# A hybrid attention layer on one core: the first half of the output projection is evicted by ScalarE, and x joins in an accumulating DMA

## The chip, the cores and the metric

The kernel runs on one core of a Trainium2 chip. A core has five engines with their own instruction queues: TensorE (PE) for matrix products, VectorE (DVE) and ScalarE (ACT) for elementwise work, GpSimd (POOL) for small elementwise work, and SyncE (SP), which here issues nearly all DMAs. Each queue runs in order; an instruction that waits holds all that stand behind it. The metric is the device time of one execution in microseconds (us); the profile comes from one execution that the hardware profiler recorded.

## What is computed

One layer of a decoder on 2048 rows of 1024 channels: an RMS norm, one input projection, three attention branches whose outputs stand side by side (512 + 256 + 256 channels), a gate, and an output projection that is added to x:

```python
def reference(x, mem, positions, ...):
    h = rms_norm(x, norm_g[l])
    proj = h @ w_in[l]
    cq, ckv, kr, dq, dk, dv, mq, z = jnp.split(proj, IN_OFFSETS, axis=-1)
    y_mla = mla_branch(...)      # 8 heads, channels 0 to 511 of y
    y_diff = diff_branch(...)    # 4 heads, 2 softmax maps each, channels 512 to 767
    y_mem = mem_branch(...)      # 4 heads against 256 memory tokens, channels 768 to 1023
    y = jnp.concatenate([y_mla, y_diff, y_mem], axis=-1) * jax.nn.silu(z)
    return x + y @ w_out[l]
```

## The kernel before

The rows are cut into 4 blocks of 512, each of 4 tiles of 128 rows. The branches run one after the other as steps: memory (m), differential (d, two groups), latent (a, four groups), each over the 4 blocks. A step is prepared (projections, norms, rotation, transposes by DMA, row maxima) and then runs its maps: scores `st` on PE (L890 to L894), the exponential on ACT (L492), its low part `plo` on DVE (L493), and the products with the values (L502 to L505). A product in full precision is three products of fp16 parts, so one [128, 512] tile of the output projection over four channel tiles of 128 is 12 matmuls (L930 to L932).

The output projection is split in two halves by channels. `out_dm` takes the four channel tiles of the differential and memory branches. For each of the 16 row tiles it loads the rows of x into a buffer `xr` (L945), adds the product to each half of it (`out_tile`, with the addition on DVE at L933), and stores it to the DRAM scratch `part` (L950). `out_a` takes the latent branch's four channel tiles for blocks 0 to 2: it loads the rows of `part` into `xa` (L960), adds the product (L933), and stores the result to `out` (L965). `xr`, `xa` and the staged rows of w_out share two buffers (tag `f4`). The last block is held on chip: `out_last` loads four tiles `acc` of `part` (L981), adds three of the four channel tiles to half of them, and `out_tail` does the rest after the last map and stores it (L1002). The products go to two PSUM tiles `pp`.

The order of the work is a list of tasks. The maps have positions in time worked out from their costs; each preparation and each filling task (`out_dm`, `out_a`, `out_last`) has a span of such positions over which it is spread by the costs that it yields. `out_dm` is spread from shortly before the first latent step to 20 positions before the fourth group, `out_a(b)` and `out_last` lie beside the last steps. Each task's instructions get a priority, and the framework puts them into the queues in an order that it takes from these priorities and a simulated timeline, so each engine's order is fixed when the kernel is built, and is made anew when an instruction changes.

Other places that the prediction speaks of: `prep_a` makes keys and queries of a latent step: POOL's memsets (L853, L859), addition (L835), rotation (L340 to L344) and power (L101), DVE's scalings (L845, L846), and SP's transposes of keys (`kT_a`, L856) and queries (`qB_a`, L864 and L873).

Of the kernel before, what the change touches and what calls it, by code (L numbers as in the profile page):

```python
# [16 lines left out]
ALU = mybir.AluOpType  # L17
# [23 lines left out]
def hybrid_block(ctx: ExitStack, tc: tile.TileContext, x, mem, positions, norm_g, w_in, mla_q_norm_g,  # L41
# [21 lines left out]

# [1 line left out]
    ident = cst.tile([P, P], BF16, name="ident")  # L65
# [37 lines left out]

# [1 line left out]
    def stage(name, pool=None):  # L105
# [10 lines left out]
    def load(dst, src, pace=PACE):  # L116
        """At the start, loads take turns with the transposes on the DMA queues."""
        if 0 < len(turned) < 2 * NPACE:
            with tc.issue_after(turned[max(0, len(turned) - pace)].ins):
                SP.dma_start(dst, src)  # L120
        else:
            SP.dma_start(dst, src)
# [18 lines left out]

# [1 line left out]
    def load_w(w, cols, gains, name, out, pool=None, ahead=2, pace=PACE):  # L143
        """Column ranges of w as fp16 pairs: NK views [P, 2, n] appended to out."""
        n = sum(c for _, c in cols)
        kpu = 2 if n > 256 else 4

        def fetch(i):
            st = stage(f"wst_{name}{i}", pool).rearrange("p (k c) -> p k c", k=2)
            at = 0  # L150
            for c0, c in cols:
                load(st[:, :, at:at + c], w[0, 2 * i * P:(2 * i + 2) * P, c0:c0 + c].rearrange("(k p) c -> p k c", p=P), pace)
                at += c
            return st

        sts = [fetch(i) for i in range(ahead - 1)]
        yield 1.0
        for i in range(NK // 2):
            if i + ahead - 1 < NK // 2:
                sts.append(fetch(i + ahead - 1))  # L160
                yield 1.0
            st = sts[i]
            if 2 * i % kpu == 0:
                wt = bigt([P, kpu, 2, 1024 // kpu], f"w_{name}{i}")
            for k in range(2):
                g = gains[:, 2 * i + k:2 * i + k + 1]
                dst = wt[:, (2 * i + k) % kpu]
                A.activation(dst[:, 0, :n], st[:, k, :n], AF.Copy, scale=g)
                V.scalar_tensor_tensor(dst[:, 1, :n], st[:, k, :n], g, dst[:, 0, :n], ALU.mult, ALU.subtract)
                out.append(dst)  # L170
            yield 1.0
# [8 lines left out]
    def project_block(hts, units, n, dst):  # L180
        """dst: [P, 4, >= n]"""
        for t in range(4):
            ps = ps_p.tile([P, 512], F32, tag="pp", name="pp")
            project(ps, hts[t], units, n)
            A.activation(dst[:, t, 0:n], ps[:, :n], AF.Copy, scale=1.0 / WS)
            yield 0.01 * n
# [6 lines left out]

# [1 line left out]
    top = tc.cur_priority  # L195
# [50 lines left out]

# [1 line left out]
    cos_t = cst.tile([P, NT, 16], F32, name="cos_t")  # L248
# [63 lines left out]
    def rope_tabs(b, g, name):  # L312
        """cos and sin of block b's tokens with the halves of the gain folded in."""
        tb = wk.tile([P, 2, 4, 32], F32, tag="rtab", name=f"rt_{name}", bufs=1)
        c = cos_t[:, 4 * b:4 * b + 4, :]
        s = sin_t[:, 4 * b:4 * b + 4, :]
        g1, g2 = _bc(g[:, 0:16], 1, 4), _bc(g[:, 16:32], 1, 4)
        G.tensor_tensor(tb[:, 0, :, 0:16], c, g1, ALU.mult)
        G.tensor_tensor(tb[:, 0, :, 16:32], c, g2, ALU.mult)
        G.tensor_tensor(tb[:, 1, :, 0:16], s, g2, ALU.mult)  # L320
        G.tensor_tensor(tb[:, 1, :, 16:32], s, g1, ALU.mult)
        return tb

    def rope(dst, src, tb, nh, eng, name):
        """dst, src: [P, 4, nh, 32]"""
        tmp = tmp4(f"rtmp_{name}")[:, 0:128 * nh].rearrange("p (t h d) -> p t h d", t=4, d=32)
        C = _bc(tb[:, 0], 2, nh)
        Sn = _bc(tb[:, 1], 2, nh)
        eng.tensor_tensor(dst, src, C, ALU.mult)
        eng.tensor_tensor(tmp[..., 0:16], src[..., 16:32], Sn[..., 0:16], ALU.mult)  # L330
        eng.tensor_tensor(tmp[..., 16:32], src[..., 0:16], Sn[..., 16:32], ALU.mult)
        eng.tensor_tensor(dst[..., 0:16], dst[..., 0:16], tmp[..., 0:16], ALU.subtract)
        eng.tensor_tensor(dst[..., 16:32], dst[..., 16:32], tmp[..., 16:32], ALU.add)

    def rope_in_place(q, tb, nh, eng, tmp):
        """q: [P, 4, nh, 32]"""
        tmp = tmp.rearrange("p (t h d) -> p t h d", t=4, d=32)
        C = _bc(tb[:, 0], 2, nh)
        Sn = _bc(tb[:, 1], 2, nh)
        eng.tensor_tensor(tmp[..., 0:16], q[..., 16:32], Sn[..., 0:16], ALU.mult)  # L340
        eng.tensor_tensor(tmp[..., 16:32], q[..., 0:16], Sn[..., 16:32], ALU.mult)
        eng.tensor_tensor(q, q, C, ALU.mult)
        eng.tensor_tensor(q[..., 0:16], q[..., 0:16], tmp[..., 0:16], ALU.subtract)
        eng.tensor_tensor(q[..., 16:32], q[..., 16:32], tmp[..., 16:32], ALU.add)  # L344

# [1 line left out]
    zsc = dr.tile([3, P, NT, 2 * P], F32, name="zsc")  # L347
# [5 lines left out]
    def put_v(vt, ps):  # L353
        """vt: [P, 2, 130], ps: [P, 2, 64] in PSUM, WS times the values"""
        A.activation(vt[:, :, 0:64], ps, AF.Copy, scale=1.0 / WS)
        V.scalar_tensor_tensor(vt[:, :, 65:129], ps, 1.0 / WS, vt[:, :, 0:64], ALU.mult, ALU.subtract)

    def put_gate(z, ps):
        """2 WS silu of the products ps"""
        A.activation(z, ps, AF.Tanh, scale=0.5 / WS)  # L360
        V.scalar_tensor_tensor(z, z, 1.0, ps, ALU.add, ALU.mult)
# [9 lines left out]

# [1 line left out]
    def est_block(st, i, nmap, mcol, lhs, rhs):  # L373
# [34 lines left out]

# [1 line left out]
    def prep_d(st, units):  # L410
# [63 lines left out]
    class Map:  # L474
        """One softmax map of one block of queries."""

# [39 lines left out]
    def finish(st, y, ct, ys, keep=False):  # L516
        """y: [P, 4, 128], already gated; its fp16 parts go out transposed."""
        b = st.b
# [63 lines left out]

# [1 line left out]
    def prep_m(st, units):  # L584
# [86 lines left out]

# [1 line left out]
    def gates(b, chunk, units):  # L673
        """2 WS silu(z) of two groups for one block, kept in DRAM."""
        for t in range(4):
# [7 lines left out]

# [1 line left out]
    krot, ss_kr = [], []  # L685
# [68 lines left out]

# [1 line left out]
    wuq, wukv = [], []  # L756
# [146 lines left out]

# [1 line left out]
    wout = {}  # L905
# [17 lines left out]
    def out_tile(yt, t, hf, acc):  # L923
        """Adds the product of the given channel tiles to one [128, 512] tile of acc."""
        ps = ps_p.tile([P, 512], F32, tag="pp", name="pp")
        tk = slice(P * t, P * t + P)
        o = slice(512 * hf, 512 * hf + 512)
        n = len(yt)
        for i, (c, y) in enumerate(yt):
            T.matmul(ps, lhsT=y[:, 0, tk], rhs=wout[c][:, 0, o], start=(i == 0), stop=False)  # L930
            T.matmul(ps, lhsT=y[:, 0, tk], rhs=wout[c][:, 1, o], start=False, stop=False)  # L931
            T.matmul(ps, lhsT=y[:, 1, tk], rhs=wout[c][:, 0, o], start=False, stop=(i == n - 1))  # L932
        V.scalar_tensor_tensor(acc, ps, 0.5 / WS, acc, ALU.mult, ALU.add)  # L933

    def out_dm():
        """x plus the products of the differential and memory channels, kept in DRAM."""
        yield from load_wout(range(4, 8))
        for b in range(NB):
# [3 lines left out]
            for t in range(4):  # L942
                i = 4 * b + t
                xr = wk.tile([P, DM], F32, tag="f4", name=f"xr{i}", bufs=2)
                SP.dma_start(xr, x[0, P * i:P * i + P, :])  # L945
                yield 0.5
                for hf in range(2):
                    out_tile(yt, t, hf, xr[:, 512 * hf:512 * hf + 512])
                    yield 2.6
# [3 lines left out]
    def out_a(b):  # L953
# [3 lines left out]
        for t in range(4):  # L957
            i = 4 * b + t
            xr = wk.tile([P, DM], F32, tag="f4", name=f"xa{i}", bufs=2)
            SP.dma_start(xr, part[:, i, :])  # L960
            yield 0.5
# [7 lines left out]
    def out_last():  # L969
        """All but the last channel tile for the last block, kept on chip."""  # L970
        b = NB - 1
# [6 lines left out]
        for t in range(4):  # L978
            acc = big.tile([P, DM], F32, tag="big", name=f"acc{t}")
            last["acc"].append(acc)  # L980
            SP.dma_start(acc, part[:, 4 * b + t, :])  # L981
            yield 0.5
# [20 lines left out]

# [1 line left out]
    zcol = 1440  # L1005
# [230 lines left out]
```

## Time and profile before

| what | value |
|---|---|
| device time, median of 3 runs | 1416.82 us (1413.11 to 1417.91) |
| span of the profiled execution | 1420.8 us |
| PE busy | 92% of the span |
| DVE busy | 79% |
| ACT busy | 63% |
| POOL busy | 25% |
| mean share of the DMA queue of SP | 47.6% of 16 engines |

The span is the time from the first to the last instruction of the profiled execution; it is a little longer than the runs without a profile. Busy shares are means over stages that differ much, so they are read with a table of stretches. A matmul's listed time includes the way through the array, so the rate of PE is read from the distance of starts. A table of waits names, for each instruction that let its engine idle, what it waited for last; an instruction of SP (SPq) that waits holds the DMAs behind it. The chain is the work that ended last, followed back from the end.

### The profile page before, as it was taken

How to read it: one execution, taken by the hardware profiler on the slowest of the kernel's cores; microseconds unless marked ns; L12 is line 12 of the kernel's file. 1: busy time of each engine (PE TensorE's matmuls, PEld its weight loads, DVE VectorE, ACT ScalarE, POOL GpSimd, SP SyncE). 2: the span in 40 equal slices, each digit the busy share in tenths (PEclk: the TensorE clock that was granted, in tenths of full speed). 3: DMA queues.
4: the chain of work that ended last, by engine and by line, in shares of the span. 5: the costliest groups of instructions: out<-in, count | busy, mean ns of one | idle time of the engine just before them, and what ended most of it. 6: DMA issues, size and time to landing. Idle time of an engine off the chain costs nothing. (4 is left out here: it accounts for less than half of the span.)

```text
span 1420.8 us, 35214 instructions
## 1 busy us (share of the span) xinstructions
PE 1312.4 (92%) x13552; PEld 831.7 (59%) x13552; DVE 1120.2 (79%) x2649; ACT 897.6 (63%) x2153; POOL 359.8 (25%) x541
## 2 busy tenths in 40 slices
PE   4789899999999999998998999999999899989998
PEld 1344456667676666677775665655655565555554
DVE  3458787889789958888899788977788999975645
ACT  5646444677777747786776676655776788664521
POOL 2222133303052044122321233533124433200000
PEclk9899999999999999999999999999999999999999
DMA  8999754223223223347245156255544454264352
GB/s 211 244 211 196 162 111 100 53 66 69 52 53 76 39 35 64 68 123 196 97 98 134 50 153 167 57 127 125 110 87 87 105 94 75 54 142 153 113 204 78
DMA packets 302696, 157.67 MB, mean 111 GB/s; under 512 B 248384, under 2 KB 281280, under 8 KB 302528
## 3 DMA queue, kind: packets, MB, share of 16 engines
q1 hardware_dynamic: 302496, 155.42, 47.6%
q8 instruction: 106, 1.74, 0.5%
q14 instruction: 62, 0.51, 0.1%
q0 software_dynamic: 32, 0.00, 0.0%
HBM read 61.79 MB, written 34.34 MB: 68 GB/s over the span
## 5 line engine op out<-in xcount | busy, mean ns | idle before, releaser
L492 ACT ACTIVATE p<-st 128x512 f32<-128x512 f32 (+3 forms) x672 | 354.6, 547 | 177.6 <-PE st L892 60.5
L493 DVE TENSOR_TENSOR plo<-p 128x512 f16<-128x512 f32 (+3 forms) x672 | 407.5, 617 | 60.1 <-ACT p L492 56.0
L505 PEld LDWEIGHTS <-plo 128*128 128x128 f16 x2304 | 217.5, 99 | 52.1 <-DVE plo L493 31.8
L502 PEld LDWEIGHTS <-p 128*128 128x128 bf16 x2304 | 219.1, 98 | 49.0 <-issue 2.3
L504 PEld LDWEIGHTS <-p 128*128 128x128 bf16 x2304 | 218.2, 98 | 29.4 <-issue 0.6
L393 ACT ACTIVATE ec<-pe 128x512 bf16<-128x512 f32 (+3 forms) x384 | 196.3, 537 | 40.5 <-PE pe L386 18.8
L394 DVE TENSOR_TENSOR er<-er,ec 128x512 bf16<-128x512 bf16 (+3 forms) x384 | 143.6, 380 | 33.5 <-ACT ec L393 20.4
L502 PE MATMUL pv<-V_d,p 128*128 128x65 f16 x1088 | 140.8, 193 | 0.8 <-DVE y_d L557 0.8
L504 PE MATMUL pv<-V_d,p 128*128 128x64 f16 x1088 | 140.7, 195 | 0.0
L502 PE MATMUL pv<-V_a,p 128*128 128x65 f16 x1088 | 139.4, 194 | 0.2
L504 PE MATMUL pv<-V_a,p 128*128 128x64 f16 x1088 | 139.2, 195 | 0.0
L505 PE MATMUL pv<-V_d,plo 128*128 128x65 f16 x1088 | 134.8, 192 | 4.5 <-DVE plo L493 3.9
L505 PE MATMUL pv<-V_a,plo 128*128 128x65 f16 x1088 | 130.6, 193 | 8.5 <-DVE plo L493 7.9
L390 ACT ACTIVATE er<-pe 128x512 bf16<-128x512 f32 x192 | 109.6, 604 | 38.3 <-DVE mx_d L399 14.2
L176 PEld LDWEIGHTS <-ht_x 128*128 128x128 f16 x896 | 88.5, 99 | 70.9 <-DMA ht_x<-xh_x 20.2
L890 PE MATMUL st<-qB_a,kT_a 97*128 97x512 f16 (+1 forms) x320 | 112.1, 350 | 18.0 <-ACT p L492 17.2
L177 PEld LDWEIGHTS <-ht_x 128*128 128x128 f16 x896 | 88.4, 99 | 55.5 <-issue 9.3
L178 PEld LDWEIGHTS <-ht_x 128*128 128x128 f16 x896 | 88.4, 99 | 54.5 <-DMA ht_x<-xl_x 4.6
L546 PE MATMUL st<-qB_d,kT_d 97*128 97x512 f16 (+1 forms) x320 | 109.2, 349 | 9.1 <-ACT p L492 8.3
L384 PE MATMUL pe<-kT_d,qB_d 96*128 96x512 f16 (+2 forms) x320 | 106.0, 350 | 8.2 <-ACT ec L393 4.7
L891 PE MATMUL st<-qB_a,kT_a 96*128 96x512 f16 (+1 forms) x320 | 112.0, 350 | 0.0
L892 PE MATMUL st<-qB_a,kT_a 96*128 96x512 f16 (+1 forms) x320 | 111.4, 348 | 0.0
(285 smaller groups left out, 3383.9 us busy)
## 6 DMA issues: line engine op xcount, KB each, us to landing
xt_x<-in_x_dram SPq DMA_DIRECT2D x16, 512.0 KB, 4.6
xr<-in_x_dram SPq DMA_DIRECT2D x16, 512.0 KB, 3.6
part<-xr SPq DMA_DIRECT2D x16, 512.0 KB, 3.0
ysc<-yt SPq DMA_DIRECT2D x31, 256.0 KB, 2.2
yl<-ysc SPq DMA_DIRECT2D x15, 512.0 KB, 4.3
zsc<-zc SPq DMA_DIRECT2D x48, 128.0 KB, 2.3
xa<-part SPq DMA_DIRECT2D x12, 512.0 KB, 3.6
out_dram<-xa SPq DMA_DIRECT2D x12, 512.0 KB, 2.7
```

The lines of the kernel that those rows point to most:

```text
L390: A.activation(er[:, t % 2], ps, AF.Copy)
L393: A.activation(ec[:, 0:n], ps[:, 0:n], AF.Copy)
L394: V.tensor_tensor(er[:, t % 2, 0:n], er[:, t % 2, 0:n], ec[:, 0:n], ALU.max)
L492: A.activation(p32[:, :n], ps[:, :n], AF.Exp, scale=self.scale)
L493: V.tensor_tensor(plo[:, :n], p32[:, :n], phi[:, :n], ALU.subtract)
L502: T.matmul(pvv[:, t, 0:65], lhsT=phi[:, c], rhs=vt[:, 0:65], start=(j == 0 and t == 0), stop=False, skip_group_check=True)
L504: T.matmul(pvv[:, t, 0:64], lhsT=phi[:, c], rhs=vt[:, 65:129], start=False, stop=False, skip_group_check=True)
L505: last["pv"] = T.matmul(pvv[:, t, 0:65], lhsT=plo[:, c], rhs=vt[:, 0:65], start=False, stop=(j == self.njt - 1), skip_group_check=True)
L546: T.matmul(ps[:, :n], lhsT=st.kTs[j // 4][0:97, h, j % 4, m % 2, :], rhs=st.qB[h][0:97, t0:4, m % 2, :], start=True, stop=not diag)
L890: T.matmul(ps[:, :n], lhsT=kt[0:97, h, j % 4, 0, :], rhs=q[0:97, 0, t0:4, :], start=True, stop=False)
L891: T.matmul(ps[:, :n], lhsT=kt[0:96, h, j % 4, 0, :], rhs=q[0:96, 1, t0:4, :], start=False, stop=False)
L892: T.matmul(ps[:, :n], lhsT=kt[0:96, h, j % 4, 1, :], rhs=q[0:96, 0, t0:4, :], start=False, stop=not diag)
```

## The change

`out_dm` no longer loads x. It copies each product out of PSUM with an ACT activation (scaled as before) into the buffer, and stores that to `part`, which now holds the products alone. Where `out_a` and `out_last` loaded rows of `part`, they now call `fetch_sum`: SP loads the rows of x into the buffer, and POOL issues a DMA that adds the rows of `part` to what is there. `out_tile` is split into the product (`out_product`) and DVE's addition, and is used by the second half as before.

```diff
     def out_tile(yt, t, hf, acc):
-        ps = ps_p.tile([P, 512], F32, tag="pp", name="pp")
...
+        ps = out_product(yt, t, hf)
+        V.scalar_tensor_tensor(acc, ps, 0.5 / WS, acc, ALU.mult, ALU.add)
+
+    def fetch_sum(dst, i):
+        SP.dma_start(dst, x[0, P * i:P * i + P, :])
+        G.dma_start(dst, part[:, i, :], accum_op=ALU.add)
+
+    def out_product(yt, t, hf):
+        ps = ps_p.tile([P, 512], F32, tag="pp", name="pp")
...
-        V.scalar_tensor_tensor(acc, ps, 0.5 / WS, acc, ALU.mult, ALU.add)
+        return ps
 
     def out_dm():
...
                 xr = wk.tile([P, DM], F32, tag="f4", name=f"xr{i}", bufs=2)
-                SP.dma_start(xr, x[0, P * i:P * i + P, :])
                 yield 0.5
                 for hf in range(2):
-                    out_tile(yt, t, hf, xr[:, 512 * hf:512 * hf + 512])
+                    ps = out_product(yt, t, hf)
+                    A.activation(xr[:, 512 * hf:512 * hf + 512], ps, AF.Copy, scale=0.5 / WS)
                     yield 2.6
                 SP.dma_start(part[:, i, :], xr)
...
     def out_a(b):
-            SP.dma_start(xr, part[:, i, :])
+            fetch_sum(xr, i)
...
     def out_last():
-            SP.dma_start(acc, part[:, 4 * b + t, :])
+            fetch_sum(acc, 4 * b + t)
```

## Rows read from the trace of the kernel before

**Rows 1.** The page: span, and busy time of each engine.
```profile
span 1420.8 us, 35214 instructions
PE 1312.4 (92%) x13552; PEld 831.7 (59%) x13552; DVE 1120.2 (79%) x2649; ACT 897.6 (63%) x2153; POOL 359.8 (25%) x541
```

**Rows 2.** Table of stretches: bounds, length, busy time by engine, granted clock, DMA.
```profile
core 0: us, PE busy (x) PEld busy (x) DVE busy (x) ACT busy (x) POOL busy (x), PEclk, DMA share, GB/s
687.00:1115.00 428.00, 395.49 (x4427) 258.57 (x4426) 362.51 (x845) 288.07 (x726) 139.46 (x216) 0.98 0.46 108
...
730.00:760.00 30.00, 28.46 (x290) 18.16 (x287) 27.59 (x63) 20.60 (x56) 13.17 (x17) 1.00 0.36 101
760.00:790.00 30.00, 25.46 (x414) 17.09 (x413) 27.37 (x74) 24.17 (x59) 1.56 (x5) 1.00 0.45 95
...
940.00:1000.00 60.00, 53.38 (x567) 34.26 (x566) 42.02 (x88) 30.22 (x77) 19.50 (x31) 0.97 0.45 109
...
1270.00:1405.00 135.00, 133.06 (x1198) 72.79 (x1199) 76.41 (x157) 50.56 (x97) 0.00 (x0) 0.99 0.43 140
```

**Rows 3.** Timeline, two neighbouring matmuls: start, duration, engine, line.
```profile
864.68 0.38 PE L932 MATMUL pp<-wo,yl 128*128 128x512 f16 x1
...
864.90 0.38 PE L930 MATMUL pp<-wo,yl 128*128 128x512 f16 x1
```

**Rows 4.** Instructions of L933 into xr: shortest/median/longest ns, first and last start.
```profile
L933 DVE SCALAR_TENSOR_TENSOR xr<-pp,xr x32: 659/679/692, 729.7 to 1086.1; 128x512 f32<-128x512 f32 x32
```

**Rows 5.** Waits in 687 to 1115: total us, times, longest.
```profile
PEld L505 <- DVE plo L493: 20.3, 40, 1.9
...
PE st L890 <- ACT p L492: 10.0, 10, 1.8
...
SPq L950 <- DVE xr L933: 30.6, 6, 10.8
SPq L945 <- DMA part<-xr: 25.7, 11, 4.6
```

**Rows 6.** Chain that ended last, 940 to 1000: shares by line, then pieces.
```profile
by line: DMA qB_a<-qs_a 13.2%; POOL r_a L101 9.7%; DMA kT_a<-ks_a 7.8%; issue 6.8%; DVE plo L493 5.3%; PE pp L930 3.5%; PE pp L931 3.2%; PE st L890 3.2%; PE pp L812 3.1%; POOL qkv_a L344 2.9%; PE st L891 2.9%; PE st L892 2.5%; PE pp L932 2.
...
964.15 0.07 DVE xr L933
...
965.41 4.68 DMA kT_a<-ks_a
```

**Rows 7.** ACT's groups: busy us, mean ns, idle before.
```profile
L390 ACT ACTIVATE er<-pe 128x512 bf16<-128x512 f32 x192 | 109.6, 604 | 38.3 <-DVE mx_d L399 14.2 <-DVE mx_a L399 12.0 <-PE pe L384 8.8
```

**Rows 8.** POOL: its one DMA issue (busy, mean ns), and its timeline after 1115.
```profile
L78 POOL DMA_DIRECT2D gm<-in_mem_norm_g_dram x1 | 1.1, 1106 | 0.0
...
1116.25 0.31 POOL L853 MEMSET ks_a<- 128x256 f16 x1 [6.19 <-DVE plo L493]
```

**Rows 9.** DMA issues: count, KB each, median us to landing.
```profile
xa<-part SPq DMA_DIRECT2D x12, 512.0 KB, 3.6
...
acc<-part SPq DMA_DIRECT2D x4, 512.0 KB, 9.7
...
gm<-in_mem_norm_g_dram POOLq DMA_DIRECT2D x1, 4.0 KB, 6.0
```

**Rows 10.** Timeline of SP: loads of xa.
```profile
1115.42 2.85 SPq L960 DMA_DIRECT2D xa<-part  x2
1279.28 0.32 SPq L960 DMA_DIRECT2D xa<-part  x1
...
1359.22 0.32 SPq L960 DMA_DIRECT2D xa<-part  x1
...
1371.71 0.32 SPq L960 DMA_DIRECT2D xa<-part  x1
```

**Rows 11.** Timeline of DVE: additions into xa.
```profile
1290.30 0.69 DVE L933 SCALAR_TENSOR_TENSOR xa<-pp,xa 128x512 f32<-128x512 f32 x1
...
1364.40 0.68 DVE L933 SCALAR_TENSOR_TENSOR xa<-pp,xa 128x512 f32<-128x512 f32 x1
...
1378.53 0.69 DVE L933 SCALAR_TENSOR_TENSOR xa<-pp,xa 128x512 f32<-128x512 f32 x1 [1.03 <-PE pp L932]
```

## The prediction

> **What bounds the kernel now.** I read the page first: PE is busy for 92% of the span, DVE for 79%, ACT for 63%, POOL for 25% [rows 1]. A share over the span hides that the change touches two different stages, so the next view is the table of busy time by stretch [rows 2]. The first half of the output projection (`out_dm`) puts its 32 products into DVE's queue between 729.7 and 1086.1 us [rows 4], inside the stretch 687 to 1115. There PE is busy for 395 of 428 us, DVE for 363, ACT for 288, POOL for 139. The second half runs from about 1270 to 1405, where PE is busy for 133 of 135 us, DVE for 76, and POOL for none.
>
> Is PE's busy time real? Matmuls are pipelined, so I look at the distance of their starts in the timeline: two neighbouring 512-column products start 0.22 us apart though each is listed with 0.38 [rows 3]. In the first stage they do stream, but between bursts there are holes: 33 us by the table. PE's weight load waits 20.3 us in 40 pieces for DVE's low part of the probabilities (L493), the scores wait 10.0 us for ACT's exponential (L492) [rows 5]. So in the first stage PE is the fullest engine, with DVE's and ACT's delays as the holes. The tail stage is PE alone: a microsecond in which PE waits there is a microsecond of the end.
>
> A third thing bounds parts of the first stage. In 940 to 1000 DVE is at its lowest (42 of 60 us), yet PE is no fuller than elsewhere (53 of 60) [rows 2]. The chain of that stretch names the preparation of the next heads: transposes of q 13.2%, of k 7.8%, the power on POOL 9.7% [rows 6]. Where this chain rules, taking work off DVE gives little; what gives is releasing the transposes in SP's queue.
>
> **Part 1: the eviction moves from DVE to ACT, in the first stage.** Removed: 32 additions at L933 of 0.679 us = 21.7 us of DVE [rows 4]. Added: 32 ACT copies of 128x512 f32 out of PSUM. The trace has the same shape into bf16, at 0.604 us [rows 7]: 32 x 0.604 = 19.3 us of ACT. Neither sum is time of the end by itself. DVE's saving lies between 6% of the 20.3 us that PE waits for DVE (21.7 of 363 us of its work) = 1.2 us, and the whole 21.7 us. I count it where DVE is the full engine: of the 30 us pieces of this stage four have DVE above 91% (730 to 790, of which the two rows stand in [rows 2], then 910 to 940 and 1060 to 1090), 120 of 428 us = 28%: 0.28 x 21.7 = -6.1 us. ACT's cost lies between nothing and 19.3 us; the cover is its idle third (288 of 428). ACT passes 80% in two pieces (760 to 790 [rows 2] and 880 to 910), 14%: +2.7 us. Behind each copy on ACT's queue stand exponentials, and PE's scores wait for those; if the copies mostly fall in front of them the cover is gone and the +2.7 goes towards 19.3. The release of the PSUM tile `pp` changes engine, not place.
>
> **Part 2: the loads of x leave `out_dm`.** 16 SP issues at L945 go. SP runs in order, and each of them reuses the buffer of the tile before last, so SP stands still until a store to `part` has landed: 25.7 us in 11 waits [rows 5]. Behind it in the queue are the transposes of the preparation. Transposes are 13.2 + 7.8 = 21% of the chain where that chain rules [rows 6]; 0.21 x 25.7 = -5.4 us. Bounds: 0 (another wait ends last) and 25.7. The store at L950 stays, and its wait on the eviction (30.6 us [rows 5]) stays with ACT in DVE's place. That this one matters too is seen at 964.15: the addition on DVE stands in the chain, and after it the transpose of k takes 4.68 us [rows 6]. I cost the exchange at nothing: the copy has no operand from DRAM, so ACT can take it as soon as the product is there; if ACT is late the same transposes wait for it.
>
> **Part 3: x comes back in the second stage.** SP issues 16 loads of x where it issued 16 loads of `part`: nothing. POOL gets 16 accumulating loads of 512 KB, each with a new wait: POOL stands until x has landed. The price is latency: each tile is ready later by e = POOL's issue plus the landing. No accumulating transfer is in the trace. Below: the one transfer that POOL issues takes 1.1 us of it [rows 8], and the plain load of the same rows lands in 3.6 us [rows 9]: e = 4.7. Above: the loads of `acc`, issued four together, land in 9.7 us [rows 9]: e = 10.8. POOL's own small load landed in 6.0 [rows 9]. I take e = 6.0, nearest to the plain load of the same bytes, with 1.3 us more since the sum has a second stream to read.
>
> Is it hidden? For `out_a`, 12 tiles take turns in two buffers. Tiles 0 and 1 are fetched from 1115 on [rows 10], long before use. For each of the other ten I take the start of the first addition less the issue of its load less 3.6 us [rows 9 to 11]: tile 2 has 1290.30 - 1279.28 - 3.6 = 7.4 us to spare, then 4.4, 5.8, 12.1, 16.3, 7.6, 7.6, and the last three 1.6 (tile 9: 1364.40 - 1359.22 - 3.6), 2.3 and 3.2 (tile 11). A late tile holds DVE's queue, with `plo` of the last heads behind it, which PE waits for. PE can cover one more product, 12 matmuls x 0.22 = 2.6 us. So the loss is the sum of e - spare - 2.6 where that is positive: at e = 4.7, 0.5 us; at 6.0, 1.8 + 1.1 + 0.2 = +3.1 us; at 10.8, 25.7 us. The four tiles `acc` have buffers of their own and are loaded ahead of the last tiles of `out_a`, which are used first; I cost them at nothing.
>
> By the Trainium skill, "DMA: Bandwidth & Descriptors", section on the anatomy of a DMA on the GpSimd path, a transfer takes about 2.0 us plus its bytes over 436 GB/s, 3.2 us for these; by that estimate e would be 4.3, the loss in the tail 0.1 us and the time 1408.6. No row here shows such a transfer of this size.
>
> The first two accumulating loads fall where the first two loads of `part` did, after 1115 [rows 10], where POOL still prepares heads. Behind them stand the memsets, the rotation and the power of L101, for which DVE's L845 and then the transposes wait. Bounds: 0 and 2 x 4.7 = 9.4 us. POOL idles there anyway (6.19 us before 1116.25 [rows 8]), so +0.5.
>
> **Sum.** -6.1 + 2.7 - 5.4 + 3.1 + 0.5 = -5.2 us on a span of 1420.8, which is 4.0 us above the median of the runs; taken from that median, 1416.8 - 5.2 = 1411.6 us.
>
> **The rivals.**
> A. The swap is neutral. DVE's load doesn't rule PE's holes (940 to 1000 speaks for it), SP then waits at the next instruction, the tail is covered: 1416.8, give or take 4. The instruction order is also made anew from a simulated timeline, so that later steps can move by microseconds either way. For it: the holes have many owners [rows 5]. Against: three of them are relieved at once.
> B. Slower: the accumulating load is the new end of the tail. Its place is the last four tiles, where PE has no other work; it decides from e = 7.7 us, at which the loss (0.7 + 3.5 + 2.8 + 1.9 = 8.9) eats the first stage's gain of 8.8. At e = 10.8: 1416.8 - 8.8 + 25.7 + 0.5 = 1434. For it: PE 133 of 135 us and 1.6 us to spare [rows 2, 10, 11]. Against: the plain load's 3.6 us.
> C. DVE really is the bound of the first stage: about two thirds of the 21.7 us show, -14.5 in place of -6.1: 1403.
> D. DVE holds up POOL's part of the transfer: each accumulating load would wait for one DVE instruction, 0.69 us [rows 11], e = 6.7, loss 2.5 + 1.8 + 0.9 = 5.2 in place of 3.1: 1413.7. Against: DVE runs 57% of the tail, so not each would meet one. The Trainium skill, "SBUF — State Buffer", section on the two sides of SBUF, has such a rule: while DVE is in a mode that uses both ports, GpSimd can't write its descriptors. It names copies and `tensor_scalar`; DVE's rows in the tail are other operations.
> That the change doesn't do what it says would be an ACT copy that waits for its buffer: 16 tiles are spread over 356 us [rows 4] and SP's wait for a store is 2.3 us on average [rows 5], so I give it no chance of its own.
>
> **How the numbers follow.** Chances: the forecast 0.36 (0.32 of it faster, 0.04 within), C 0.08, A 0.30 (0.26 within, 0.04 slower), B 0.24 (0.22 slower, 0.02 within), D 0.02 (within). About 0.3% or 4.3 us is what a measurement of this kernel can tell from no change, so faster means under 1412.6. Together: faster 0.40, same 0.34, slower 0.26. The range reaches down past C to 1401 and up into B, to e of about 9.7 us, 1427. The forecast's own range is 1405 to 1414.
>
> **What would show it.** In the trace of the changed kernel: DVE's busy time down by some 22 us and ACT's up by 19, both before 1115; no wait of SP on `part<-xr` ahead of a load; PE's waits on L493 in that stage under 20.3 us. In the tail: the time to landing of POOL's transfers (e under 7.7 for a gain), and no idle time of DVE ahead of L933 that ends with a DMA. Wrong it is if those waits end with the DMA, if PE's scores wait for ACT much longer than 10 us, or if the span between the first stage's start and 1270 doesn't shrink.

## The result, and the profile after

The changed kernel takes 1452.3 us (median of 4 runs, 1440.7 to 1458.4) where the kernel before took 1416.9 beside it: 1.024 times as long, 95% interval 1.020 to 1.028. Forecast was 1411.6, in a range of 1401 to 1427. The profiled execution has a span of 1447.3 us, 26.5 more than the one of before, so the trace shows most of the 35 us.

The page of the changed kernel, as [rows 1]:

```profile
span 1447.3 us, 35253 instructions
PE 1311.5 (91%) x13552; PEld 831.9 (57%) x13552; DVE 1101.4 (76%) x2617; ACT 912.9 (63%) x2185; POOL 371.0 (26%) x557
```

The work moved as meant: DVE has 18.8 us less, ACT 15.3 more, PE the same. So the loss is idle time in the main. Where it lies is read from the first and the last start of the steps of the output projection. First the kernel before, then the changed one (columns: count, shortest/median/longest ns, first and last start in us):

```profile
L933 DVE SCALAR_TENSOR_TENSOR xa<-pp,xa x24: 660/691/693, 1273.5 to 1383.4; 128x512 f32<-128x512 f32 x24
L933 DVE SCALAR_TENSOR_TENSOR acc<-pp,acc x16: 682/692/692, 1388.4 to 1417.2; 128x512 f32<-128x512 f32 x16
```
```profile
L957 ACT ACTIVATE xr<-pp x32: 576/597/762, 729.0 to 1087.5; 128x512 f32<-128x512 f32 x32
L926 DVE SCALAR_TENSOR_TENSOR xa<-pp,xa x24: 658/691/693, 1284.2 to 1413.4; 128x512 f32<-128x512 f32 x24
L926 DVE SCALAR_TENSOR_TENSOR acc<-pp,acc x16: 683/691/693, 1416.9 to 1443.6; 128x512 f32<-128x512 f32 x16
```

The first half ends at 1087.5 where it ended at 1086.1 [rows 4]: nothing won, 1.4 us lost. The second half begins 10.7 us later. From its first addition to the last one into `acc` I call the tail: it was 143.7 us long and is now 159.4. So there are two losses, one of some 11 us ahead of the tail and one of 16 us in it.

The table of stretches, to be held against [rows 2]: in the first stage PE is no fuller than before (392 of 428 us against 395) although DVE has 21 us less to do; in the second, PE, which had 2 us of idle time in 135, has 16 in 144.

```profile
687.00:1115.00 428.00, 392.12 (x4413) 257.06 (x4411) 341.41 (x802) 300.71 (x752) 138.75 (x217) 0.99 0.38 86
...
1270.00:1414.00 144.00, 128.29 (x1170) 70.41 (x1169) 74.61 (x166) 54.34 (x107) 12.57 (x15) 0.95 0.71 189
```

The tail alone, before and after:

```profile
1273.50:1417.20 143.70, 142.17 (x1241) 76.55 (x1239) 83.12 (x165) 49.53 (x95) 0.00 (x0) 1.00 0.41 137
```
```profile
1284.20:1443.60 159.40, 145.04 (x1240) 77.38 (x1238) 81.34 (x164) 49.53 (x96) 12.26 (x14) 0.96 0.63 171
```

PE stood idle for 1.5 us of the tail before and stands for 14.4 now. Its busy time grew too, from 142.2 to 145.0 us, for the same work: the mean granted clock was 1.00 and is 0.96. Of the clock's two levels, 2.4 and 1.2 GHz, PE had the lower one for 3.4 us after a wait of 2.6 us that ended at 1328.0, and for 10.2 us that began within its longest wait and ended at 1400.5. After that wait matmuls of 512 columns start some 0.43 us apart, where they start 0.22 us apart in [rows 3]:

```profile
1397.63 0.59 PE L939 MATMUL pp<-wo,yl 128*128 128x512 f16 x1 [8.97 <-DVE xa L926]
1398.01 0.63 PE L940 MATMUL pp<-wo,yl 128*128 128x512 f16 x1
1398.44 0.63 PE L941 MATMUL pp<-wo,yl 128*128 128x512 f16 x1
```

Waits of the first stage, as [rows 5] (total us, times, longest):

```profile
PEld L505 <- DVE plo L493: 13.3, 30, 1.9
...
PE st L890 <- ACT p L492: 13.1, 10, 3.3
...
SPq L959 <- ACT xr L957: 50.1, 11, 11.1
```

PE waits 7.0 us less for DVE and 3.1 more for ACT. SP's waits ahead of the loads of x (25.7 us) are gone with the loads, but SP now stands 50.1 us for ACT's copy where it stood 30.6 for DVE's addition, with the same transposes behind it.

Waits of the tail, 1270 to 1425:

```profile
POOL xa L931 <- DMA xa<-in_x_dram: 42.1, 5, 10.7
DVE xa L926 <- DMA xa<-part: 31.7, 5, 9.6
...
PE pp L939 <- DVE xa L926: 12.2, 3, 9.0
...
SPq L930 <- DMA out_dram<-xa: 43.3, 9, 10.7
```

Before, no addition of the second half waited for a DMA. Now five wait 31.7 us for the accumulating load, and PE stands 12.2 us because both `pp` tiles hold products that DVE hasn't taken. The chain that ended last shows one round of a buffer, store, load of x, accumulating load, addition (start, duration):

```profile
1295.22 5.27 DMA out_dram<-xa
1300.51 3.99 DMA xa<-in_x_dram
...
1305.04 8.70 DMA xa<-part
...
1313.82 0.69 DVE xa L926
```

From the landing of x (1304.50) to that of the sum (1313.74) is 9.2 us: this is the e of the prediction. Taken in the same way for each of the ten tiles, e was 5.9 to 6.2 us six times, 8.7, 9.2 and 9.4 us once each, and 12.3 us for tile 9 (the twelve tiles of `out_a` are counted from 0). PE's 12.2 us are mostly this one tile: 9.0 us stand before its product, 2.6 and 0.6 before two others. POOL had issued the four accumulating loads of `acc` just ahead of that of tile 9, which took 11.7 us to land (1385.14 to 1396.86):

```profile
1375.97 0.87 POOL L931 DMA_DIRECT2D acc<-part  x1 [10.92 <-PE pp L941]
...
1381.02 0.87 POOL L931 DMA_DIRECT2D acc<-part  x1 [0.38 <-issue]
1385.14 0.87 POOL L931 DMA_DIRECT2D xa<-part  x1 [3.25 <-DMA xa<-in_x_dram]
...
1396.88 1.29 DVE L926 SCALAR_TENSOR_TENSOR xa<-pp,xa 128x512 f32<-128x512 f32 x2 [9.61 <-DMA xa<-part]
```

The clock also has a part in the whole time. The four runs of the changed kernel had a mean granted clock of 0.972 to 0.980. The nine runs of the kernel before that stand beside the first experiments had 0.981 to 0.989, with 1412.1 us at 0.989 and 1422.0 us at 0.982; over these nine, 0.001 of the clock goes with about 0.9 us. So some 8 of the 35 us, as an estimate from these runs, go with the lower clock; the two profiled executions, at 0.982 and 0.980, differ by 26.5 us. How much of that would stay if PE's holes were gone isn't shown; the tail's 2.9 us followed its holes.

### The profile page after: what moved, and what is told of

Its sections match the earlier page's. It is cut to its first block, busy times and chain, and to the rows that moved or that the text cites. A ratio compares the mean times of both kernels' runs of the same rounds, so it can differ in the third digit from the quotient of the medians.

```text
span 1447.3 us, 35253 instructions
## 1 busy us (share of the span) xinstructions
PE 1311.5 (91%) x13552; PEld 831.9 (57%) x13552; DVE 1101.4 (76%) x2617; ACT 912.9 (63%) x2185; POOL 371.0 (26%) x557
## 5 line engine op out<-in xcount | busy, mean ns | idle before, releaser
L390 ACT ACTIVATE er<-pe 128x512 bf16<-128x512 f32 x192 | 110.4, 608 | 30.6 <-DVE mx_d L399 13.1
L384 PE MATMUL pe<-kT_a,qB_a 96*128 96x512 f16 (+2 forms) x320 | 100.4, 354 | 21.1 <-DMA qB_a<-qs_a 9.9
L891 PE MATMUL st<-qB_a,kT_a 96*128 96x512 f16 (+1 forms) x320 | 112.3, 351 | 0.0
```

The lines of the kernel that those rows point to most:

```text
L384: T.matmul(ps[:, 0:n], lhsT=lhs(m, t), rhs=rhs(m, c, n // P), start=True, stop=c < b)
L390: A.activation(er[:, t % 2], ps, AF.Copy)
L891: T.matmul(ps[:, :n], lhsT=kt[0:96, h, j % 4, 0, :], rhs=q[0:96, 1, t0:4, :], start=False, stop=False)
```

## The experiments

**The two halves apart.** In the first kernel only the first half is changed; x is never added.

```diff
     def fetch_sum(dst, i):
-        SP.dma_start(dst, x[0, P * i:P * i + P, :])
-        G.dma_start(dst, part[:, i, :], accum_op=ALU.add)
+        SP.dma_start(dst, part[:, i, :])
```

> Only the first half of the change: ACT copies the products out without x, and the second half loads the rows of part alone, by SP as in the kernel before. x is never added, so that no load of x stands in either half. Theory 1 (the loss is the longer chain of loads behind each reused buffer in the second half): the loss is gone, 1408 to 1418 us, and the second half has the kernel-before's waits, DVE never waiting for a DMA ahead of its addition. Theory 2 (ACT's copies and the order made anew from them cost the 9 us that the changed kernel lost between 1115 and 1270 us): about 1425 us or more, with the first addition into xa at about 1284 us where the kernel before has 1273.5.

1427.9 us, 1.008 [1.005, 1.011] of the kernel before: 11 us slower, with the whole second half as it was. Its additions:

```profile
L926 DVE SCALAR_TENSOR_TENSOR xa<-pp,xa x24: 660/692/693, 1276.0 to 1384.8; 128x512 f32<-128x512 f32 x24
L926 DVE SCALAR_TENSOR_TENSOR acc<-pp,acc x16: 683/692/693, 1389.8 to 1418.6; 128x512 f32<-128x512 f32 x16
```

The tail is 142.6 us long, so its loss is gone, as theory 1 wanted. The time is theory 2's, but not its place: the first addition comes at 1276.0, not at 1284, and the profiled execution (a span of 1422.6 us, 5 under the median) shows little of the 11 us. They don't come from the second half, and no wait stands for them. Nor does the clock explain them: its runs had 0.983 in the mean, those of the kernel before 0.985.

The second kernel has only the second half changed (`out_dm` loads x and adds it on DVE as before, so x counts twice).

> Only the second half of the change: the first half adds x on DVE as before, and the second half loads x by SP and adds part by POOL's accumulating DMA, so x is in the sum twice. Theory 1 (the chain of loads): the whole loss or nearly so, 1440 to 1455 us, DVE waiting some 30 us for the accumulating loads. Theory 2 (the first half's share): 1435 us, about 9 us less than the changed kernel.

1436.1 us, 1.013 [1.009, 1.018]. The time is that of theory 2. DVE waits 27.5 us for the accumulating loads, PE 9.3 us before the product of tile 9 again, and the tail is 156.7 us long. These are 19.5 of the 35 us, and the tail's 13 are among them.

**The adding, in the same order.** POOL's load overwrites the rows of x (so x is missing); the plan sees no difference, and the queues of all five engines hold the same instructions in the same order as in the changed kernel.

```diff
-        G.dma_start(dst, part[:, i, :], accum_op=ALU.add)
+        G.dma_start(dst, part[:, i, :])
```

> The changed kernel with POOL's load as a plain one, which overwrites the rows of x: the same two loads, waits and queues, without the adding, so x is missing from the sum. If the price is the second load in the chain whatever it does, its median time to landing is about 5 us and three quarters of the loss stay: 1438 to 1450 us. If the price is the adding itself, the second load lands in under 4 us, and the time is 1420 to 1432 us.

1438.0 us: 14.3 less than the changed kernel, whose own runs lie 18 us apart, with nothing but the adding left out. The time is at the lower edge of the first reading, and the landing of 4.2 us lies between the two; the tail decides. Its additions, then two of its waits (1285 to 1439):

```profile
L926 DVE SCALAR_TENSOR_TENSOR xa<-pp,xa x24: 664/691/692, 1291.8 to 1404.0; 128x512 f32<-128x512 f32 x24
L926 DVE SCALAR_TENSOR_TENSOR acc<-pp,acc x16: 683/692/692, 1408.5 to 1435.2; 128x512 f32<-128x512 f32 x16
```
```profile
DVE xa L926 <- DMA xa<-part: 17.3, 5, 5.0
...
PE pp L939 <- DVE xa L926: 1.3, 1, 1.3
```

Its DMA issues in 1270 to 1425 (KB each, median us to landing), then those of the changed kernel in the same stretch:

```profile
out_dram<-xa SPq DMA_DIRECT2D x12, 512.0 KB, 3.5
xa<-in_x_dram SPq DMA_DIRECT2D x10, 512.0 KB, 4.1
xa<-part POOLq DMA_DIRECT2D x10, 512.0 KB, 4.2
```
```profile
out_dram<-xa SPq DMA_DIRECT2D x12, 512.0 KB, 4.2
xa<-in_x_dram SPq DMA_DIRECT2D x10, 512.0 KB, 3.7
xa<-part POOLq DMA_DIRECT2D x10, 512.0 KB, 5.6
```

The tail is 143.4 us long, as before. So the second load in the chain is hidden: DVE waits 17.3 us for it, but never more than 5.0 at once, and PE loses 1.3. The accumulating load lands 1.4 us later in the median, POOL takes 0.87 us to issue it in place of 0.53, and the stores land later too. The gap is widest at tile 9, whose load took 5.4 us here, behind four plain loads of `acc`, and 11.7 us with the adding; there DVE's wait of 9.6 us was more than PE could cover. The loss that stays (21 us) lies ahead of the tail: its first addition is at 1291.8, 7.6 us later than in the changed kernel, though the order is the same. From 1115 to the tail the granted clock was 0.94 here and 0.98 there, which is some 20 us at the lower level against 7. As an estimate, the 13 us more at half the rate are up to 7 us of PE's time, so most of this difference can be the clock of the one execution that was profiled.

**Other buffers.** The tiles `xa` in the pool of large buffers, so that no fetch waits for the store of the tile before last.

```diff
-            xr = wk.tile([P, DM], F32, tag="f4", name=f"xa{i}", bufs=2)
+            xr = big.tile([P, DM], F32, tag="big", name=f"xa{i}")
```

> The changed kernel with the tiles xa of the second half in the pool of 22 large buffers in place of the two staging buffers, so that a fetch needn't wait for the store of the tile before last. Theory 1 (latency behind a reused buffer): the additions no longer wait for DMAs and most of the 20 us that were lost after 1284 us come back: 1418 to 1432 us. Theory 3 (the accumulating transfers slow all the others, stores and loads alike, whatever the buffers): above 1440 us, with stores still at 4 us and DVE still waiting for the loads.

1438.0 us, above what theory 1 wanted and below what theory 3 wanted. Its first fetch of `xa`, and its additions:

```profile
L930 SPq DMA_DIRECT2D xa<-in_x_dram x12: 422/427/737, 1273.7 to 1360.7; - x12
L926 DVE SCALAR_TENSOR_TENSOR xa<-pp,xa x24: 680/691/693, 1289.9 to 1396.0; 128x512 f32<-128x512 f32 x24
L926 DVE SCALAR_TENSOR_TENSOR acc<-pp,acc x16: 682/692/692, 1401.5 to 1430.2; 128x512 f32<-128x512 f32 x16
```

Its accumulating loads among the DMA issues of 1250 to 1425, then two of its waits (1270 to 1434):

```profile
xa<-part POOLq DMA_DIRECT2D x12, 512.0 KB, 12.7
```
```profile
DVE xa L926 <- DMA xa<-part: 13.7, 2, 9.3
...
PE pp L939 <- DVE xa L926: 6.4, 2, 3.2
```

The tail is 140.3 us, shorter than in the kernel before, though with so many under way the accumulating loads land in 12.7 us. Part of the shortness is that the first addition itself came 4.3 us late while PE had gone on. PE's waits for DVE are halved, to 6.4 us, and the long one before tile 9 is gone: so the reused buffer is much of what makes the loads dear. The other reading, that slower transfers cost time whatever the buffers, isn't refuted: two additions, at 1289.9 and 1325.9, still waited 13.7 us. The start was late: the first fetch was issued at 1273.7, where the two staging buffers could be filled from 1115 on.

**Is it the order?** The 11 us of the first half had no owner in the waits. First, DVE copies out in ACT's place, without x:

```diff
-                    A.activation(xr[:, 512 * hf:512 * hf + 512], ps, AF.Copy, scale=0.5 / WS)
+                    V.tensor_scalar_mul(xr[:, 512 * hf:512 * hf + 512], ps, 0.5 / WS)
```

> As the kernel with only the first half changed, but DVE copies the products out in ACT's place (x is never added). It keeps the removal of the loads of x and takes the move to ACT back. If the move to ACT costs the 11 us that the first half lost, this is at the kernel before's time or under it, 1408 to 1418 us. If it is the order made anew, anything within 12 us of the kernel before, and DVE's busy time back at 1120 us.

1426.5 us, 1.006 [1.004, 1.009]: about as slow as with ACT, so the 11 us don't need the move to ACT (the order is made anew here too). SP's wait for the eviction in 687 to 1115, first in this kernel, then in the kernel with only the first half changed and 2.5 in its plan (below):

```profile
SPq L958 <- DVE xr L956: 31.4, 7, 11.2
```
```profile
SPq L958 <- ACT xr L956: 30.4, 7, 11.9
```

Both are as in the kernel before (30.6), so the 50.1 us of the changed kernel belong to its order, not to ACT. Then the kernel before itself, with one number of its plan changed, which alters no instruction, only the order in which the queues hold them:

```diff
                     out_tile(yt, t, hf, xr[:, 512 * hf:512 * hf + 512])
-                    yield 2.6
+                    yield 2.5
```

> The kernel before with one number of its plan changed: the first half's tasks count 2.5 positions for a product in place of 2.6. Every instruction is the same, only the order of the queues is made anew. If the order alone moves the time as much as the first half's change did, it differs from the kernel before by 5 us or more, either way; if the order is of no consequence, it is within 3 us.

1431.0 us, 1.009 [1.006, 1.012]. An order made anew cost 12 us with nothing else changed. The same number in the kernel with only the first half changed:

> The kernel with only the first half changed, with the same other number of the plan (2.5 in place of 2.6). If the 11 us were a matter of the order, the time moves by 5 us or more against 1428; if they belong to ACT's copies, it stays at 1424 to 1432 us, and 8 to 14 us above the kernel before with that number.

1422.5 us, 8.5 under the kernel before with that number: the sign is turned round. I then took the same number through 2.4 to 2.8.

> The kernel before with 2.7 positions for a product of the first half in its plan: another order of the same instructions. Theory 1 (the order made anew moves the time by itself): anywhere from 1410 to 1435 us. Theory 2 (the order is of little consequence, and 2.5 was an exception): 1414 to 1421 us.

> Only the first half of the change (x is never added), with 2.7 in the plan. Beside the kernel before with 2.7 it gives a third pair, after +9 us at 2.6 and -8.5 us at 2.5. If the first half has a price or gain of its own, the mean of the three keeps one sign by several us; if it has none, the pair differs either way within 12 us and the mean is near 0.

> The changed kernel with 2.7 in the plan. Against the kernel with only the first half at 2.7 it gives the price of the second half in another order: theory 1 (the chain of loads behind a reused buffer) 18 to 30 us, as the 24 us at 2.6, whatever the order; if the order rules this too, from 5 to 40 us.

> The changed kernel with 2.5 in the plan. Against the kernel with only the first half at 2.5 (1422.5 us) theory 1 wants 18 to 30 us more, 1440 to 1453 us; if the order rules, from 1428 to 1460.

> The kernel before with 2.4 positions for a product of the first half in its plan. If the kernel before has an unusually good order at 2.6, this is slower by 8 us or more: 1425 us and above. If 2.5 and 2.7 were the exceptions, within 5 us of 1417.

> Only the first half of the change (x is never added), with 2.4 in the plan: a fourth pair. If the first half gains by itself about what was predicted (-8.8 us), it is 4 to 18 us under the kernel before with 2.4. If the order alone decides, either sign.

> The kernel before with 2.8 in the plan, as with 2.4: slower by 8 us or more if 2.6 is an unusually good order, within 5 us of 1417 if not.

> Only the first half of the change (x is never added), with 2.8 in the plan: a fifth pair. 4 to 18 us under the kernel before with 2.8 if the first half has a gain of its own; either sign if the order alone decides.

Medians in us (each was run beside the kernel before, whose medians were 1416.5 to 1418.9):

| number in the plan | kernel before | first half only | difference | whole change | second half |
|---|---|---|---|---|---|
| 2.4 | 1418.5 | 1417.6 | -0.9 | not run | |
| 2.5 | 1431.0 | 1422.5 | -8.5 | 1438.7 | +16.2 |
| 2.6 (as given) | 1416.5 | 1427.9 | +11.4 | 1452.3 | +24.4 |
| 2.7 | 1441.0 | 1425.6 | -15.4 | 1446.3 | +20.7 |
| 2.8 | 1416.9 | 1418.6 | +1.7 | not run | |

Two readings follow. The first half's effect is -2.3 us in the mean of five orders, between -15.4 and +11.4; the differences scatter by some 10 us, so a gain of its own is not shown, and neither is a loss. At the good orders (2.4 and 2.8) both kernels stand at the same 1417 to 1419. That the kernel before owes its time to an unusually lucky order, as I had come to think, isn't so either: three of its five orders give that time. The second half costs 16 to 24 us in each of the three orders tried.

What it costs beyond the 16 us of the tail can in part be seen where the first two accumulating loads stand, after 1115. In the changed kernel PE stands 4.5 us there, and with 2.7 in the plan 11.3 us; the longest such wait is 2.2 us in the kernel before. The pieces of the chain, first in the changed kernel with PE after it, then with 2.7:

```profile
1129.03 7.26 DMA qB_a<-qs_a
...
1136.34 1.03 PE L384 MATMUL pe<-kT_a,qB_a 96*128 96x512 f16 x2 [4.54 <-DMA qB_a<-qs_a]
```
```profile
1115.22 15.21 DMA kT_a<-ks_a
```

These transposes were in flight together with POOL's loads (landing in 7.3 and 6.8 us, and in 15.7 and 14.3). With 2.5 in the plan the two loads landed in 5.4 and 6.2 us, the one transpose issued beside them took 2.8, PE stood for at most 2.4 us, and the second half cost no more than the tail. In the kernel with the plain load a transpose took 8.4 us at this place and PE stood 6.0 us, so it isn't the adding. This fits the excess, but no run moves the two loads away by themselves.

The profiles also show which part of the time moves with the order. The additions of the kernel before at 2.7, its slowest order, and of the changed kernel at 2.5, its fastest:

```profile
L933 DVE SCALAR_TENSOR_TENSOR xa<-pp,xa x24: 660/691/692, 1293.0 to 1401.8; 128x512 f32<-128x512 f32 x24
L933 DVE SCALAR_TENSOR_TENSOR acc<-pp,acc x16: 683/692/692, 1406.8 to 1435.6; 128x512 f32<-128x512 f32 x16
```
```profile
L926 DVE SCALAR_TENSOR_TENSOR xa<-pp,xa x24: 659/690/692, 1270.4 to 1399.1; 128x512 f32<-128x512 f32 x24
L926 DVE SCALAR_TENSOR_TENSOR acc<-pp,acc x16: 683/691/693, 1402.6 to 1429.3; 128x512 f32<-128x512 f32 x16
```

The tail is 142.6 us here and 158.9 there. In the ten profiles of the kernel before and of the first half only it is 142.5 to 143.7 us, in the three of the whole change 158.9 to 159.4. What the order moves is where the tail begins: 1266 to 1293 in the kernel before.

**The accumulating transfer where nobody waits at once.** x is copied into `part` ahead, POOL's accumulating store adds the products in the first half, and the second half loads `part` alone.

```diff
+        SP.dma_start(part, x[0].rearrange("(i p) c -> p i c", p=P))
...
-                SP.dma_start(part[:, i, :], xr)
+                G.dma_start(part[:, i, :], xr, accum_op=ALU.add)
```

> The changed kernel with the accumulating DMA moved to where nobody waits for it at once: one DMA copies x into part ahead of the first half, POOL's accumulating store adds the products that ACT copied out, and the second half loads part by SP alone, as in the kernel before. If the chain of loads in the second half is the loss that remains beside the first half's own, this gives the time of the kernel with only the first half, 1428 us, give or take 6, with no wait of DVE for a load in the second half. If POOL's waits for the copies hold up the preparation of the heads, 1440 us or more.

1467.9 us. The copy waits for nothing, so it was put at 28 us, beside the loads at the start, and ACT's first copy of a product came at 759.4 in place of 729.0. In the next try the copy was made tile by tile, to be issued after ACT's copy of the tile before:

```diff
+                with tc.issue_after(last["turn"].ins):
+                    SP.dma_start(part[:, i, :], x[0, P * i:P * i + P, :])
```

> As the earlier try with the accumulating store in the first half, but the rows of x go into part tile by tile, DRAM to DRAM, each behind ACT's copy of the tile before. The second half loads part by SP alone. If an accumulating transfer that nobody waits for is free, the time is that of the kernels with only the first half changed, 1422 to 1430 us, with no idle time of DVE that ends with a load in the second half; if POOL's place in the preparation of the heads makes it dear, 1436 us or more.

> The same kernel with 2.5 in the plan: 1418 to 1430 us if the accumulating store is free, 1436 us or more if it isn't.

1454.7 and 1470.0 us, and again not what was meant: the copies still ran at the start.

```profile
L954 SPq DMA_DIRECT2D part<-in_x_dram x16: 490/562/718, 27.9 to 72.2; - x16
```
```profile
L926 DVE SCALAR_TENSOR_TENSOR xa<-pp,xa x24: 661/692/693, 1300.8 to 1409.4; 128x512 f32<-128x512 f32 x24
L926 DVE SCALAR_TENSOR_TENSOR acc<-pp,acc x16: 683/692/693, 1414.5 to 1443.2; 128x512 f32<-128x512 f32 x16
```

Of these three kernels one thing can be used: their tails are 142.9, 142.4 and 142.6 us long. An accumulating transfer ahead of the tail leaves the tail alone. Whether it is free in the first stage stays open: from ACT's first copy to the first addition of the tail they take 558, 555 and 573 us where the kernels with only the first half changed take 547, and the place of POOL's waits and the order made anew aren't told apart.

## Why the prediction was wrong

Two terms failed above all. The tail was to lose 3.1 us and lost 15.7, because one e of 6.0 us stood for every tile and the four fetches of `acc` were costed at nothing. And the first half of the change was to gain 8.8 us, of which the runs show nothing that is clear of their scatter.

- **The exchange of 21.7 us of DVE for 19.3 us of ACT** was sized rightly (0.601 us for a copy, 0.604 taken from [rows 7]), and PE's waits for DVE fell from 20.3 to 13.3 us as the prediction wanted. The step that failed is the next one, which turned the share of the stage in which DVE is full into -6.1 us: PE was no fuller there, 392 us against 395. Five pairs show -2.3 us in the mean for the whole first half. They scatter too much to exclude -8.8 by themselves, but at either kernel's good orders there is no gain. The rows of 940 to 1000, where less DVE work meant no fuller PE [rows 2], were in hand and were given to the rival.
- **The removal of SP's waits, -5.4 us**, failed because SP then waited at other instructions, as rival A says. By the table of waits, all of them in 687 to 1115 add up to 350 us before and 361 in the changed kernel. The store's longer wait for ACT (50.1 us against 30.6), whose exchange was costed at nothing, isn't needed for that: where DVE copies out, that wait is 31.4 us and the waits ahead of the loads of x are gone, yet the sum is 355 us and the time 1426.5.
- **The accumulating load** was the right mechanism with the wrong size. Six of ten tiles had about the e of 6.0 us that was taken, four had more; most of the loss is in tile 9 with e = 12.3, which stood behind and beside the four accumulating loads of `acc`. With the ten measured values of e, the prediction's own sum of lateness gives 11.7 us (2.2 + 0.3 + 8.1 + 1.0 + 0.2), and PE waited 12.2 us for DVE; slower matmuls at the lower clock add 2.9. So rival B was at work, at chance 0.24, and mostly at its place: 9.6 of the 12.2 us lie in the last four tiles, 2.6 at the addition at 1327. Three more profiles with accumulating loads into the two staging buffers have the same single wait of 9.2 to 9.3 us, the one without the adding has 1.3. Whether the loads of `acc` alone make tile 9 late isn't shown, as no run takes them away.
- **The cover of 2.6 us** isn't one number. Waits of DVE of 6.5, 7.5 and 6.1 us (tiles 3, 4 and 11) cost PE 0, 2.6 and 0.6 us directly, but the 9.6 us of tile 9 cost 9.0.
- **The first two accumulating loads, +0.5 us**, were costed by POOL's idle time alone. The transposes that were in flight with them were left out; in the changed kernel PE stood 4.5 us for one.
- **The order made anew** stood in rival A as plus or minus 4 us. Measured with no instruction changed it is 0 to +23 us in the kernel before (1441.0 beside 1417.7 at 2.7). Of the 35 us, about 16 are the adding in the tail, shown by the kernel in the same order and by all profiles; the rest lies ahead of the tail. In that part the first half's new order accounts for some 11 us, shown as a difference between orders, not as a wait that could be named; what more the second half costs there (24.4 - 16) fits the late transposes and isn't settled.
- **By the Trainium skill**, "DMA: Bandwidth & Descriptors", section on the anatomy of a DMA on the GpSimd path, 2.0 us plus the bytes over 436 GB/s gives an estimate of 3.2 us for a transfer of this size. The trace doesn't agree: it has 4.2 us for the plain load and 5.6 for the accumulating one in the median, beside other traffic. The measurement decides, and the time of 1408.6 us that went with the estimate is out.
- **Rival D** has little for it: POOL's plain loads, beside the same instructions of DVE in the same order, left the tail as it was, and the accumulating issues took 0.85 to 0.96 us throughout in the changed kernel. The lateness is in the landing. (Three rows of DVE in the tail are `tensor_scalar` after all, at L407.)

No version here beats the kernel before: the best others (its own order at 2.8, 1416.9 us, and at 2.4) are the same within the interval. The change with large buffers and an early first fetch wasn't tried.

## What to carry to other kernels

A step that lengthens a load is costed on the whole round of its buffer, store, load and second load together, and each transfer in that round is taken at what it will be when the queues carry more. Look for the place where the most transfers meet: here four fetches with buffers of their own, costed at nothing, stood ahead of the one tile that lost most. Work that is taken off a queue's wait is a gain only if the queue doesn't wait at its next instruction instead, so add up all its waits. Where the order of the queues is made anew from a plan, first run the unchanged kernel with a number of the plan moved a little: here that alone was worth up to 23 us, more than any term of the sum, and one timing of a change says as much on the order as on the change. A stretch whose start moves with the order but whose length doesn't, like the tail here, is a better measure of one mechanism than the time of the whole.

## What the hardware showed

An accumulating load of 512 KB from DRAM landed in 5.6 us (median of ten in the tail, the longest 11.7) where a plain one from the same queue, in the same order, took 4.2; POOL's issue took 0.87 against 0.53 us. Beside it the stores of 512 KB landed in 4.2 us, against 3.5 beside the plain loads and 2.7 in the kernel before, one of them in 11.1 us (the store at 1377.23) while four accumulating loads of `acc` were under way; with plain ones the store at that place took 9.4 us.

A transpose by SP that was in flight with POOL's first two loads of 512 KB took 7.3, 9.7 and 15.2 us in three kernels with accumulating loads (the changed one, that with only the second half changed, and the changed one at 2.7) and 8.4 us with plain ones; beside SP's two loads of `part` in the kernel before it took 4.3. Not every one was slow: in the changed kernel the transpose issued 0.8 us ahead of the first load took 4.4.

The granted clock fell to 1.2 GHz for 3.4 us after PE had waited 2.6 us, and for 10.2 us around a wait of 9.0 us; matmuls of 512 columns then started 0.43 us apart in place of 0.22.
